# A third projection block behind the x loop, and the end of a search behind the fourth head

## The chip, the cores and the metric

The kernel runs on one core of a Trainium2 chip. A core has TensorE (PE, matmuls), VectorE (DVE), ScalarE (ACT), GpSimd (POOL) and SyncE (SP, which here issues nearly all DMAs); each works through its own queue in order, and they wait for each other by semaphores. The metric is device time in microseconds (us) of one execution.

## The reference

One inference step of a hybrid decoder layer, for 512 prompt tokens and 8 x 8 sample tokens (T = 576 in all), model width 2048. One projection feeds two branches: sparse attention, in which an indexer chooses the 256 keys each token may see, and gated linear attention (GLA). Both are gated and go through an output projection.

```python
def index_scores(qi, wi, ki):
    dots = jnp.einsum('bthd,bsd->btsh', qi, ki) * (D_IDX ** -0.5)
    return jnp.einsum('btsh,bth->bts', jax.nn.relu(dots), wi)
...
z = jnp.einsum('btd,de->bte', rms_norm(x, norm_in), w_in)        # split into q, k, v, gate, indexer q, k, w, GLA parts
_, idx = lax.top_k(jnp.where(causal, index_scores(qi, wi, ki), -jnp.inf), topk)
s = jnp.where(valid, q @ k[idx], NEG_BIG)                        # prompt: keys of the prompt
o = softmax(s) @ v[idx]                                          # sample: keys in a paged cache, and the new ones
y = rms_norm(x + concat([o * silu(ga), gla_out * silu(gb)]) @ w_out, norm_f)
```

## The kernel before

**Products.** All of it is float32, and each product is made of three matmuls of rounded parts: `w_hi*x_hi + w_lo*x_hi + w_hi*x_lo`. `wload` brings one weight piece (128 x 512, 256 KB): a DMA on SP into `w_raw` (3 buffers), a cast on ACT to `w_hi` (L180), a subtraction on DVE, in some stages on POOL, to `w_lo` (L183); `w_hi` and `w_lo` have 5 buffers each. `gemm(b)` projects 128 output columns from four such pieces: 16 slices of the model width, three products each. `kmm` makes all 576 tokens as two matmuls of 288 columns per product, `kmm_q` only 448 tokens in one matmul of 448 columns. Result tiles are `ps_g` (2 buffers of PSUM); `mm1` gives a tile of a second PSUM pool (`pm`, 3 buffers).

**Stages.** First the x loop (L272 on): x comes in 16 pieces, and blocks 0 (small columns: indexer key, indexer weights, GLA rank) and 1 (first indexer query) are accumulated as it comes. Behind it stands what depends on their sums: `raw0` copies block 0's sum out (L280), `rope64` swaps rows of block 1's sum into `ev_sw` by four copies on ACT (L293), the indexer key becomes `kih`/`kil` (L343, L344), and `pw` transposes the indexer weights on TensorE (L349). Then eight indexer blocks (`idx_block`), each with a query projection, `rope64` and six score matmuls `pq` (L419, L420). `squares` (L367) sums the squares of x, for the norm, on ACT: one 1 MB load `xt` and one instruction of 2048 columns per indexer block. Then heads 0 to 7 of the prompt attention (`head`): query, key, value and gate projections, scores, softmax, and `head_out` with transposes `pt`, the split `th`/`tl` (L721, L722), products `pv` and the gated result `ga` (L727). Heads 0 and 4 also project a group of values (`vgroup`).

**Work woven in.** The search for the top keys (prompt, then sample: `topk_sample`) is a generator `bg`, advanced a few steps at marked places of heads 0 to 3; what is left is drained behind head 3. Its end (L546 to L563) merges two halves of the sample search and writes the mask `biasS`. After that the tiles of the search give their memory to a pool in which `units` loads key and value pages (`kt`, `vt`, 5 tiles of four 256 KB loads) and computes the sample attention `pS`, `pOs` in pieces between the projections of heads 4 to 7. GLA, gates and the output projection follow.

**Order.** A scheduler, and not the program text alone, sets each engine's queue: it takes the instructions by priority and by its own model of times. `tc.high_priority(offset=WOFF)` puts weight loads ahead, `tc.issue_after(x)` keeps an instruction behind x in that order. `rounded` collects the `w_hi` casts, `ended` the last matmul of a chain.

Of the kernel before, what the change touches and what calls it, by code (L numbers as in the profile page):

```python
# [16 lines left out]
ALU = mybir.AluOpType  # L17
# [3 lines left out]
P = 128  # L21
# [98 lines left out]
def build(tc, I, O):  # L120
# [11 lines left out]
    def v2(ap):  # L132
        return ap.rearrange("p (j t) -> p j t", j=2)
# [67 lines left out]
    def split_x(k):  # L201
# [16 lines left out]
        xh.append(h)  # L218
        xl.append(l)

    def kmm(ps, k, hi, lo):
        wh = hi[:, (k % 4) * P : (k % 4 + 1) * P]
        wl = lo[:, (k % 4) * P : (k % 4 + 1) * P]
        for n, (wt, xt) in enumerate(((wh, xh[k]), (wl, xh[k]), (wh, xl[k]))):
            for j in range(2):
                pe.matmul(  # L226
                    ps[:, j, :HT], wt, xt[:, j * HT : (j + 1) * HT],
                    start=(k == 0 and n == 0), stop=(k == NK - 1 and n == 2),
                )

    def kmm_q(ps, k, hi, lo):
        c = slice((k % 4) * P, (k % 4 + 1) * P)
        for n, (wt, xt) in enumerate(((hi, xh[k]), (lo, xh[k]), (hi, xl[k]))):
            pe.matmul(ps[:, 0, :TQ], wt[:, c], xt[:, P:T], start=(k == 0 and n == 0), stop=(k == NK - 1 and n == 2))  # L234

    def gemm(b, mm=kmm, ps=None):
        if ps is None:
            ps = pg.tile([P, 2, 512], F32, name="ps_g", tag="ps_g")
        for half in range(2):
            for k0 in (8 * half, 8 * half + 4):  # L240
                hi, lo = wload(I["w"][b, :, k0 : k0 + 4, :])
                for k in range(k0, k0 + 4):
                    mm(ps, k, hi, lo)
            fill()
        return ps[:, :, :HT] if mm is kmm else ps[:, 0, :TQ]
# [10 lines left out]
    def mm1(name):  # L256
        return pm.tile([P, 512], F32, name=name, tag="pm")

    ended = []

    def run(first, *rest):
        lead = first()
        with tc.issue_after(getattr(lead, "ins", lead)), tc.high_priority(offset=WOFF):
# [10 lines left out]
    for k in range(NK):  # L274
        split_x(k)
        for b in range(2):
            _, hi, lo = first_w[b, k // 4]
            (kmm_q if b else kmm)(psf[b], k, hi, lo)
    raw0 = sm.tile([P, T], F32, name="raw0", tag="vaS")
    se.copy(v2(raw0), psf[0][:, :, :HT])  # L280
    ps0 = v2(raw0)

    ident = cload("ident", P, P)
# [5 lines left out]
    def rope64(ps):  # L289
        sw = ev.tile([P, TQ], F32, name="ev_sw", tag="e0", bufs=2)  # L290
        for q4 in range(4):
            d4 = q4 ^ 1
            se.copy(sw[32 * d4 : 32 * d4 + 32], ps[32 * q4 : 32 * q4 + 32])  # L293
        t1 = ev.tile([P, TQ], F32, name="ev_t1", tag="e1", bufs=2)
        ve.tensor_tensor(out=t1, in0=ps, in1=C64[:, P:T], op=ALU.mult)
        po_.tensor_tensor(out=sw, in0=sw, in1=S64[:, P:T], op=ALU.mult)
        ve.tensor_tensor(out=t1, in0=t1, in1=sw, op=ALU.add)
        return t1
# [47 lines left out]
    se.activation(v2(wiT), ps0[96:112], AF.Copy, scale=1.0 / 32.0)  # L346
    pw = mm1("pw")
    for i in range(1, 4):
        pe.transpose(pw[:, 16 * i : 16 * i + 16], wiT[:, P * i : P * (i + 1)], ident[0:16, 0:16])  # L349
    wtok = pa.tile([P, 48], F32, name="wtok")  # L350
    ve.tensor_copy(wtok, pw[:, 16:64])
    rstd = cp.tile([P, T], F32, name="rstd")
# [50 lines left out]
    sc = [None] + [pb.tile([P, (256, 384, 520)[i - 1]], F32, name=f"sc{i}", tag=f"sc{i}")[:, : P * (i + 1)] for i in range(1, 4)]  # L403

    def idx_block(blk):
        t1 = rope64(gemm(1 + blk, kmm_q, mm1("ps_q").rearrange("p (o n) -> p o n", o=1) if blk == 1 else None)) if blk else t1_first
        for e in range(2):
            hh = 2 * blk + e
            r = slice(64 * e, 64 * e + 64)
            rl_ = slice(64 - 64 * e, 128 - 64 * e)  # L410
            qs = pa.tile([P, TQ], F32R, name="qis", tag=("qis", "kch")[e], bufs=2)
            se.copy(qs[r], t1[r])
            ve.tensor_tensor(out=qs[rl_], in0=t1[r], in1=qs[r].bitcast(F32), op=ALU.subtract)
            po_.tensor_copy(qiS[:, :, hh, :], qs[:, TP - P :].bitcast(F32).rearrange("p (b t) -> p b t", t=DT))
            for i in range(1, 4):
                n = P * (i + 1)
                pq = mm1("pq")
                qc = slice(P * (i - 1), P * i)
                pe.matmul(pq[:, :n], qs[:, qc], kih[:, :n], start=True, stop=False)  # L419
                pe.matmul(pq[:, :n], qs[:, qc], kil[:, :n], start=False, stop=True)  # L420
                rl = pa.tile([P, 512], F32, name="rl", bufs=8)
                se.activation(rl[:, :n], pq[:, :n], AF.Relu)
                wcol = wtok[:, 16 * (i - 1) + hh : 16 * (i - 1) + hh + 1]
                if hh == 0:
                    ve.tensor_scalar(out=sc[i], in0=rl[:, :n], scalar1=wcol, scalar2=None, op0=ALU.mult)
                else:
                    ve.scalar_tensor_tensor(out=sc[i], in0=rl[:, :n], scalar=wcol, in1=sc[i], op0=ALU.mult, op1=ALU.add)

    for blk in range(8):
        idx_block(blk)  # L430
        if blk == 1:
            for to, src in ((ptab, "page_table"), (bm, "k_bm"), (gnorm, "gla_norm"), (bgate, "b_gate")):
                with tc.issue_after(wloads[-1]):
                    sy.dma_start(to, I[src])
        if blk == 6:
            raw = pr.tile([P, D], F32, name="xt", bufs=2)
            with tc.issue_after(wloads[-3]):
                sy.dma_start(raw[:, :512], I["k_sel"])
                sy.dma_start(raw[:, 512:960], I["k_lm"])
            po_.tensor_copy(selw, raw[:, :512])  # L440
            po_.tensor_copy(lm, raw[:, 512:960])
        if 0 < blk < 6:
            squares(blk - 1)
        if blk == 5:
            token_scales()
    for i in range(1, 4):
        n = P * (i + 1)
# [83 lines left out]
    def topk_sample():  # L531

        K = 256
        wk = pb.tile([P, T], F32, name="wk", tag="wk")[:, : 512 + DT]
        top = pb.tile([P, 256], F32, name="top", tag="sc1")
        turned = pb.tile([P, 384], F32, name="turned", tag="sc2")[:, :K]
        yield from topk(sS, K, wk, top, turned)
        far = pb.tile([P, K], F32, name="far")
        for r0 in range(0, P, 32):
            for to in (0, 16):  # L540
                sy.dma_start(far[r0 + to : r0 + to + 16], turned[r0 + 16 - to : r0 + 32 - to])

        u, cnt = wk[:, :K], pb.tile([P, 8], F32, name="cnt")
        by8 = lambda x: x.rearrange("p (r e) -> p e r", e=8)
        for e in range(8):
            ve.tensor_tensor(out=by8(u)[:, e], in0=by8(top)[:, e], in1=by8(far)[:, 7 - e], op=ALU.max)  # L546
        thr = cnt[:, 0:1]
        ve.tensor_reduce(out=thr, in_=u, op=ALU.min, axis=AX.X)

        for c, (src, op) in enumerate(((top, ALU.is_gt), (far, ALU.is_gt), (far, ALU.is_equal))):  # L550
            ve.tensor_scalar(out=u, in0=src, scalar1=thr, scalar2=None, op0=op)
            ve.reduce_sum(out=cnt[:, c + 1 : c + 2], in_=u, axis=AX.X)
        ve.scalar_tensor_tensor(out=cnt[:, 4:5], in0=cnt[:, 3:4], scalar=bm[:, 5:6], in1=cnt[:, 1:2], op0=ALU.mult, op1=ALU.add)
        ve.tensor_tensor(out=cnt[:, 4:5], in0=cnt[:, 4:5], in1=cnt[:, 2:3], op=ALU.add)
        ve.tensor_scalar(out=cnt[:, 4:5], in0=cnt[:, 4:5], scalar1=-1.0, scalar2=float(K), op0=ALU.mult, op1=ALU.add)
        rank = pb.tile([P, 520], F32, name="rank", tag="sc3")
        ve.tensor_scalar(out=wk, in0=sS, scalar1=thr, scalar2=None, op0=ALU.is_equal)
        ve.tensor_tensor_scan(out=rank, data0=wk, data1=wk, initial=0.0, op0=ALU.add, op1=ALU.max)
        ve.scalar_tensor_tensor(out=wk, in0=rank, scalar=cnt[:, 4:5], in1=wk, op0=ALU.is_le, op1=ALU.mult)
        ve.scalar_tensor_tensor(out=wk, in0=sS, scalar=thr, in1=wk, op0=ALU.is_gt, op1=ALU.add)  # L560
        ve.tensor_scalar(out=wk, in0=wk, scalar1=-1.0, scalar2=-NEG, op0=ALU.add, op1=ALU.mult)
        po_.tensor_copy(biasS[:, :512], wk[:, :512])
        ve.tensor_tensor(  # L563
            out=biasS[:, 512:].rearrange("p (b s) -> p b s", b=NB), in0=own.rearrange("p (b s) -> p b s", b=NB),
            in1=wk[:, 512:].unsqueeze(1).to_broadcast([P, NB, DT]), op=ALU.min,
        )
        yield
# [143 lines left out]
    def head_out(h, Pi, v, g1):  # L711
        vh, vl = v
        pv = mm1("pv")
        for j in range(4):
# [9 lines left out]
            pe.matmul(pv[:, P * j :], vh[:, vc], th[:, :n], start=(j == 0), stop=False)  # L724
            pe.matmul(pv[:, P * j :], vl[:, vc], th[:, :n], start=False, stop=False)
            pe.matmul(pv[:, P * j :], vh[:, vc], tl[:, :n], start=False, stop=(j == 3))
        ve.tensor_tensor(out=g1[:, :TP], in0=pv, in1=g1[:, :TP], op=ALU.mult)  # L727
        sy.dma_start(spill_a[h], g1[:, :TP])

    def head(h, bg, n):  # L730
# [160 lines left out]
    head(2, bg, 4)  # L891
    head(3, bg, 4)
    lo_eng[0] = ve
    for _ in bg:
        pass
    pb_s.close()
    pc_s.close()
    un, un_s = pool("unit", 1, side="right")
# [542 lines left out]
```

## Time and profile before

| | |
|---|---|
| median of 3 runs | 1231.33 us (1230.85 to 1232.21) |
| the profiled execution, and its span | 1230.99 us, 1229.2 us |
| granted TensorE clock, mean | 0.995 |
| busy in the span | PE 1210.2 us (98%), DVE 658.9, ACT 563.4, POOL 298.2 |
| chain that ended last | PE 91%, DVE 5%, ACT 2%, the rest 1% or less each |

The span is what the profile covers, 1.8 us less than the execution. A matmul's busy time overlaps the next one's, so TensorE's throughput is read from the distance between starts. A number in brackets behind a row is idle time before it, with the instruction that ended it. The granted clock is 1.00 at full speed (2.4 GHz) and 0.50 at half.

### The profile page before, as it was taken

To read this page: it belongs to the slowest core of one execution; us is meant where nothing else is said; L and a number is where in the kernel's file an instruction comes from. 1 tells how busy PE (TensorE), PEld (TensorE's weight loads), DVE (VectorE), ACT (ScalarE), POOL (GpSimd) and SP (SyncE) were. 2 spreads that over 40 slices of the span, in tenths; PEclk is the share of its full clock that TensorE was granted. 3 is DMA by queue.
4 is the path that set the end of the run, shared out by engine and by line. 5 is a ranking of instruction groups with operands and counts; after the bars stand their busy time and mean duration, and the time that the engine had idled before them with its cause. 6 is when DMAs were issued, how large, how long until landed. Compare 5 with 4: busy or idle time off the path is not lost.

```text
span 1229.2 us, 23550 instructions
## 1 busy us (share of the span) xinstructions
PE 1210.2 (98%) x8693; PEld 1073.7 (87%) x8693; DVE 658.9 (54%) x1328; ACT 563.4 (46%) x1077; POOL 298.2 (24%) x472
## 2 busy tenths in 40 slices
PE   8799999999999999999999999999999999999997
PEld 8799997899998779998888788788899998888897
DVE  6577899789863413444344535435465562323233
ACT  6686565445443423353334453445466542222234
POOL 1124656545420210100101420402223010101021
PEclk9899999999999999999999999999999999999999
DMA  9543334422376578656356693776425454334245
GB/s 312 171 152 98 100 90 113 158 78 93 102 258 206 178 257 282 226 167 228 113 199 228 219 339 125 265 256 218 151 83 188 152 167 140 103 103 122 80 125 176
DMA packets 127157, 209.55 MB, mean 170 GB/s; under 512 B 14513, under 2 KB 38082, under 8 KB 126338
## 3 DMA queue, kind: packets, MB, share of 16 engines
q1 hardware_dynamic: 125890, 206.50, 51.2%
q10 hardware_dynamic: 1152, 1.55, 0.4%
q8 instruction: 68, 1.11, 0.4%
q14 instruction: 47, 0.39, 0.1%
HBM read 184.65 MB, written 23.22 MB: 169 GB/s over the span
## 4 chain that ended last, share of the span: by engine, by line
PE 91%; DVE 5%; ACT 2%; issue 1%; DMA 1%; POOL 1%; SPq 0%; DVEq 0%; POOLq 0%; ACTq 0%
PE ps_g L226 38%; PE ps_g L234 6%; PE acc L1286 5%; PE acc L1284 5%; PE acc L1285 5%; PE ps_g L629 4%; PE ps_g L630 4%; PE ps_g L631 4%; PE pOs L265 2%; PE pS L265 1%; PE acc L1289 1%; PE acc L1288 1%; DVE wk L518 1%; PE ps_v L626 1%; PE ps_v L625 1%
## 5 line engine op out<-in xcount | busy, mean ns | idle before, releaser
L180 ACT CAST w_hi<-w_raw 128x512 fp32r<-128x512 f32 x316 | 193.9, 619 | 363.2 <-PE ps_g L226 122.7
L183 DVE TENSOR_TENSOR w_lo<-w_raw,w_hi 128x512 fp32r<-128x512 f32 x252 | 178.3, 710 | 322.9 <-ACT w_hi L180 314.5
L226 PE MATMUL ps_g<-xh,w_hi 128*128 128x288 f32 x1312 | 289.7, 299 | 0.5 <-ACT xh L215 0.5
L226 PE MATMUL ps_g<-xl,w_hi 128*128 128x288 f32 x1312 | 289.0, 299 | 0.0
L226 PE MATMUL ps_g<-xh,w_lo 128*128 128x288 f32 x1312 | 285.7, 297 | 0.0
L226 PEld LDWEIGHTS ps_g<-xh,w_hi 128*128 128x128 f32 x1312 | 213.6, 189 | 5.8 <-issue 1.7
L226 PEld LDWEIGHTS ps_g<-xl,w_hi 128*128 128x128 f32 x1312 | 213.3, 189 | 2.4 <-issue 1.2
L226 PEld LDWEIGHTS ps_g<-xh,w_lo 128*128 128x128 f32 x1312 | 212.3, 188 | 0.7
L1285 PE MATMUL acc<-w_lo,mh 128*128 128x512 f32 (+1 forms) x320 | 110.7, 346 | 0.0
L1286 PE MATMUL acc<-w_hi,ml 128*128 128x512 f32 (+1 forms) x320 | 110.7, 346 | 0.0
L1284 PE MATMUL acc<-w_hi,mh 128*128 128x512 f32 (+1 forms) x320 | 110.3, 346 | 0.0
L183 POOL TENSOR_TENSOR w_lo<-w_raw,w_hi 128x512 fp32r<-128x512 f32 x64 | 86.4, 1352 | 63.8 <-ACT w_hi L180 55.6
L629 PE MATMUL ps_g<-w_hi,xh 128*128 128x512 f32 x256 | 101.4, 397 | 0.2 <-DVE ev_t L592 0.2
L630 PE MATMUL ps_g<-w_lo,xh 128*128 128x512 f32 x256 | 100.4, 392 | 0.0
L631 PE MATMUL ps_g<-w_hi,xl 128*128 128x512 f32 x256 | 99.8, 390 | 0.0
L1285 PEld LDWEIGHTS acc<-w_lo,mh 128*128 128x128 f32 x320 | 60.5, 189 | 7.5
L1286 PEld LDWEIGHTS acc<-w_hi,ml 128*128 128x128 f32 x320 | 60.4, 189 | 7.5
L1284 PEld LDWEIGHTS acc<-w_hi,mh 128*128 128x128 f32 x320 | 60.4, 189 | 7.5
L1308 POOL TENSOR_TENSOR y<-y,nfb 128x512 f32<-128x512 f32 (+1 forms) x20 | 22.3, 1126 | 178.6 <-ACT yjk L1304 178.4
L629 PEld LDWEIGHTS ps_g<-w_hi,xh 128*128 128x128 f32 x256 | 48.1, 188 | 12.2 <-issue 1.7
L631 PEld LDWEIGHTS ps_g<-w_hi,xl 128*128 128x128 f32 x256 | 48.1, 188 | 9.9
L630 PEld LDWEIGHTS ps_g<-w_lo,xh 128*128 128x128 f32 x256 | 48.1, 188 | 9.7
(358 smaller groups left out, 1943.5 us busy)
## 6 DMA issues: line engine op xcount, KB each, us to landing
w_raw<-in_w SPq DMA_DIRECT2D x188, 256.0 KB, 3.0
kt<-in_ck SPq DMA_DIRECT2D x128, 256.0 KB, 5.2
vt<-in_cv SPq DMA_DIRECT2D x128, 256.0 KB, 5.3
w_raw<-in_wv SPq DMA_DIRECT2D x64, 256.0 KB, 3.0
w_raw<-in_wo SPq DMA_DIRECT2D x64, 256.0 KB, 2.7
xr<-in_xT SPq DMA_DIRECT2D x15, 288.0 KB, 4.9
xt<-in_xp SPq DMA_DIRECT2D x4, 1024.0 KB, 7.1
sv<-v_tok SPq DMA_DIRECT2D x16, 256.0 KB, 5.2
```

What stands on the lines that cost most here:

```text
L180: c = se.copy(hi, raw)
L183: lo_eng[0].tensor_tensor(out=lo, in0=raw, in1=hi.bitcast(F32), op=ALU.subtract)
L226: pe.matmul(ps[:, j, :HT], wt, xt[:, j * HT : (j + 1) * HT], start=(k == 0 and n == 0), stop=(k == NK - 1 and n == 2),)
L234: pe.matmul(ps[:, 0, :TQ], wt[:, c], xt[:, P:T], start=(k == 0 and n == 0), stop=(k == NK - 1 and n == 2))
L265: last = f()
L629: pe.matmul(accs[i], xh[k][:, c], wh, start=a, stop=False)
L630: pe.matmul(accs[i], xh[k][:, c], wl, start=False, stop=False)
L631: pe.matmul(accs[i], xl[k][:, c], wh, start=False, stop=b)
L1284: pe.matmul(acc, mh[k][:, tsl], wh, start=(k == 0), stop=False)
L1285: pe.matmul(acc, mh[k][:, tsl], wl, start=False, stop=False)
L1286: pe.matmul(acc, ml[k][:, tsl], wh, start=False, stop=(k == NK - 1))
L1308: po_.tensor_tensor(out=yc[:, :m], in0=yc[:, :m], in1=nfb[r, c0 : c0 + m], op=ALU.mult)
```

## The change

Two parts. In the first, the projection of block 2 (`gemm(2)`), which `idx_block(1)` used to ask for, is written directly behind the x loop. The copies `raw0` and `ev_sw` are kept behind the last cast of the block's weights (`rounded[-1]`), and the transposes `pw` behind the last matmul of the last `kmm_q` block (`ended[0]`). `squares`, `token_scales` and one load of constants move one indexer block later. In the second, `topk_sample` has four empty steps more, so that its end is left to the drain, and the drain is kept behind the last `ga` product (`px["end"]`), that of head 3.

```diff
+    ended = []
@@ kmm_q
-            pe.matmul(ps[:, 0, :TQ], wt[:, c], xt[:, P:T], start=(k == 0 and n == 0), stop=(k == NK - 1 and n == 2))
+            m = pe.matmul(ps[:, 0, :TQ], wt[:, c], xt[:, P:T], start=(k == 0 and n == 0), stop=(k == NK - 1 and n == 2))
+        ended[:] = [getattr(m, "ins", m)]
@@ behind the x loop
+    ps_next = gemm(2, kmm_q, mm1("ps_q").rearrange("p (o n) -> p o n", o=1))
     raw0 = sm.tile([P, T], F32, name="raw0", tag="vaS")
-    se.copy(v2(raw0), psf[0][:, :, :HT])
+    with tc.issue_after(rounded[-1]):
+        se.copy(v2(raw0), psf[0][:, :, :HT])
@@ rope64
-            se.copy(sw[32 * d4 : 32 * d4 + 32], ps[32 * q4 : 32 * q4 + 32])
+            with tc.issue_after(rounded[-1]):
+                se.copy(sw[32 * d4 : 32 * d4 + 32], ps[32 * q4 : 32 * q4 + 32])
@@ pw
-        pe.transpose(pw[:, 16 * i : 16 * i + 16], wiT[:, P * i : P * (i + 1)], ident[0:16, 0:16])
+        with tc.issue_after(ended[0]):
+            pe.transpose(pw[:, 16 * i : 16 * i + 16], wiT[:, P * i : P * (i + 1)], ident[0:16, 0:16])
@@ idx_block and the loop over it
-        t1 = rope64(gemm(1 + blk, kmm_q, mm1("ps_q").rearrange("p (o n) -> p o n", o=1) if blk == 1 else None)) if blk else t1_first
+        t1 = rope64(ps_next if blk == 1 else gemm(1 + blk, kmm_q)) if blk else t1_first
-        if blk == 6:
+        if blk == 7:
...
-        if 0 < blk < 6:
-            squares(blk - 1)
-        if blk == 5:
+        if 1 < blk < 7:
+            squares(blk - 2)
+        if blk == 6:
             token_scales()
@@ topk_sample
         yield from topk(sS, K, wk, top, turned)
+        for _ in range(4):
+            yield
@@ head_out
-        ve.tensor_tensor(out=g1[:, :TP], in0=pv, in1=g1[:, :TP], op=ALU.mult)
+        m = ve.tensor_tensor(out=g1[:, :TP], in0=pv, in1=g1[:, :TP], op=ALU.mult)
+        px["end"] = getattr(m, "ins", m)
@@ behind head(3, bg, 4)
-    for _ in bg:
-        pass
+    with tc.issue_after(px["end"]):
+        for _ in bg:
+            pass
```

In TensorE's queue before, the end of the x loop (`ps_g_102` and `ps_g_103` are the sums of blocks 0 and 1, `ps_g_698` is block 3):

```order
L226 MATMUL ps_g_102<-xl_408,w_hi_345 128x288 x2
L234 MATMUL ps_g_103<-xl_408,w_hi_351 128x448
L349 MATMUL pw_505<-c_ident_422,sS_503 128x16 x3
L234 MATMUL ps_g_698<-xh_120,w_hi_701 128x448
L234 MATMUL ps_g_698<-xh_120,w_lo_703 128x448
```

The same place now (`ps_q_420` is block 2, `ps_g_695` block 3), with block 2's last three slices left out:

```order
L228 MATMUL ps_g_102<-xl_408,w_hi_345 128x288 x2
L236 MATMUL ps_g_103<-xh_407,w_hi_351 128x448
L236 MATMUL ps_g_103<-xh_407,w_lo_352 128x448
L236 MATMUL ps_g_103<-xl_408,w_hi_351 128x448
L236 MATMUL ps_q_420<-xh_200,w_hi_441 128x448
L236 MATMUL ps_q_420<-xh_200,w_lo_443 128x448
...
L236 MATMUL ps_q_420<-xl_408,w_hi_477 128x448
L236 MATMUL ps_g_695<-xh_120,w_hi_698 128x448
L236 MATMUL ps_g_695<-xh_120,w_lo_700 128x448
L236 MATMUL ps_g_695<-xl_121,w_hi_698 128x448
L355 MATMUL pw_578<-c_ident_495,sS_576 128x16 x3
```

The 48 matmuls of block 2 stood behind the first `pq`; now 12 stand inside the x loop's last slices, 36 right behind it, and `pw` behind these and three of block 3.

In ScalarE's queue before, from the last cast within the x loop on:

```order
L180 CAST w_hi_586<-w_raw_584 128x512
L280 COPY raw0_420<-ps_g_102 128x576
L180 CAST w_hi_604<-w_raw_602 128x512
L293 COPY ev_sw_434<-ps_g_103 32x448 x4
L335 COPY ev_sw_491<-raw0_420 32x576
L336 COPY ev_sw_491<-raw0_420 32x576
L346 ACTIVATE sS_503<-raw0_420 16x576
L180 CAST w_hi_622<-w_raw_620 128x512
L367 ACTIVATE xt_695,sst_512<-xt_695 128x2048
L180 CAST w_hi_701<-w_raw_699 128x512
```

And now:

```order
L180 CAST w_hi_441<-w_raw_439 128x512
L180 CAST w_hi_459<-w_raw_457 128x512
L180 CAST w_hi_477<-w_raw_475 128x512
L180 CAST w_hi_698<-w_raw_696 128x512
L284 COPY raw0_493<-ps_g_102 128x576
L298 COPY ev_sw_507<-ps_g_103 32x448 x4
L340 COPY ev_sw_564<-raw0_493 32x576
L341 COPY ev_sw_564<-raw0_493 32x576
L351 ACTIVATE sS_576<-raw0_493 16x576
L180 CAST w_hi_716<-w_raw_714 128x512
```

All casts of block 2 and the first of block 3 (`w_hi_698`) now stand ahead of the copies; the square sum stands three casts later, ahead of `kih`.

In VectorE's queue now, behind head 3's `ga` (before, the rows L546 to L563 stood between the `tl` of head 2, ahead of that head's `ga`):

```order
L730 TENSOR_TENSOR tl<-pt,th 128x128
L183 TENSOR_TENSOR w_lo<-w_raw,w_hi 128x512
L735 TENSOR_TENSOR ga<-pv,ga 128x512
L554 TENSOR_TENSOR wk<-top,far 128x32 x8
L600 TENSOR_TENSOR ev_t_4824<-ps_g,c_c_1520 128x576
L556 TENSOR_REDUCE cnt<-wk 128x1
...
L569 TENSOR_SCALAR wk<-wk 128x520
L183 TENSOR_TENSOR w_lo<-w_raw,w_hi 128x512
L571 TENSOR_TENSOR biasS<-c_own,wk 128x64
L600 TENSOR_TENSOR ev_t_5015<-ps_g,c_c_1520 128x576
```

Between `ga` and `biasS` stand, besides the search's end, four `w_lo` and head 4's query (`ev_t_4824`, `ql`); head 4's key (`ev_t_5015`) follows. In SP's queue 20 `kt` loads now follow each other behind eight pieces of the value group's weights, where before they were spread between weight loads of head 3.

## Rows read from the trace of the kernel before

**Rows 1.** Waits of TensorE, whole span: engine, tile, line, releaser; us, times, longest
```profile
PE pw L349 <- ACT sS L346: 5.3, 1, 5.3
...
PE pv L726 <- DVE tl L722: 1.5, 1, 1.5
```
**Rows 2.** Timeline of TensorE, x loop's end: start, us, instruction, idle before, releaser
```profile
29.12 0.36 PE L234 MATMUL ps_g<-xl,w_hi 128*128 128x448 f32 x1
34.81 0.50 PE L349 MATMUL pw<-c_ident,sS 16*128 16x16 f32 x3 [5.33 <-ACT sS L346]
37.86 0.74 PE L234 MATMUL ps_g<-xh,w_hi 128*128 128x448 f32 x1 [2.55 <-ACT w_hi L180]
...
41.70 0.36 PE L234 MATMUL ps_g<-xh,w_hi 128*128 128x448 f32 x1
```
**Rows 3.** Windows: length; busy PE, PEld, DVE, ACT, POOL; granted clock; DMA share; GB/s
```profile
20.00:30.00 10.00, 9.49 (x60) 8.84 (x58) 6.66 (x13) 6.30 (x13) 0.00 (x0) 1.00 1.02 335
...
36.00:38.00 2.00, 0.14 (x1) 0.14 (x1) 1.17 (x3) 2.00 (x4) 0.00 (x0) 0.50 0.83 296
```
**Rows 4.** Timeline of ScalarE, same place
```profile
29.32 0.64 ACT L280 COPY raw<-ps_g 128x576 f32<-128x576 f32 x1 [3.22 <-PE ps_g L226]
...
30.55 2.13 ACT L293 COPY ev_sw<-ps_g 32x448 f32<-32x448 f32 x4
...
34.08 0.68 ACT L346 ACTIVATE sS<-raw 16x576 f32<-16x576 f32 x1
...
35.31 1.91 ACT L367 ACTIVATE xt<-xt 128x2048 f32<-128x2048 f32 x1
...
38.89 0.67 ACT L343 CAST kih<-wk 64x576 fp32r<-64x576 f32 x1
```
**Rows 5.** DMA issues, 18 to 50 us: KB each, median us to landing
```profile
xt<-in_xp SPq DMA_DIRECT2D x3, 1024.0 KB, 7.3
w_raw<-in_w SPq DMA_DIRECT2D x9, 256.0 KB, 4.5
```
**Rows 6.** Timeline of VectorE, the sample search's end
```profile
330.03 1.01 DVE L546 TENSOR_TENSOR wk<-top,far 128x32 f32<-128x32 f32 x7
...
343.29 0.23 DVE L563 TENSOR_TENSOR biasS<-c_own,wk 128x64 bf16<-128x64 f32 x1
```
**Rows 7.** Timeline of the DMA queue of SyncE: first page loads
```profile
346.10 1.41 SPq L157 DMA_DIRECT2D kt<-in_ck  x3
...
348.18 2.98 SPq L157 DMA_DIRECT2D kt<-in_ck  x5
```
**Rows 8.** Timeline of TensorE: projections, first page scores, head 3's last product
```profile
375.44 0.42 PE L226 MATMUL ps_g<-xh,w_hi 128*128 128x288 f32 x2
375.70 0.42 PE L226 MATMUL ps_g<-xh,w_lo 128*128 128x288 f32 x2
...
379.92 0.62 PE L262 MATMUL pS<-kt,qz 128*32 128x512 f32 x1
...
383.77 0.28 PE L726 MATMUL pv<-tl,vh 128*128 128x128 f32 x1
...
396.71 0.40 PE L629 MATMUL ps_g<-w_hi,xh 128*128 128x512 f32 x1
396.95 0.39 PE L630 MATMUL ps_g<-w_lo,xh 128*128 128x512 f32 x1
```
**Rows 9.** Windows while pages are loaded, columns as in Rows 3
```profile
346.00:352.00 6.00, 6.00 (x48) 6.00 (x47) 1.44 (x3) 2.51 (x4) 2.57 (x7) 1.00 0.70 237
352.00:356.00 4.00, 4.00 (x33) 4.00 (x32) 2.60 (x4) 1.25 (x2) 1.90 (x2) 1.00 1.03 391
```
**Rows 10.** DMA issues of the whole run
```profile
kt<-in_ck SPq DMA_DIRECT2D x128, 256.0 KB, 5.2
```
**Rows 11.** Windows of VectorE alone: length, busy (instructions), clock, DMA share, GB/s
```profile
150.00:160.00 10.00, 9.83 (x21) 1.00 0.16 49
```
**Rows 12.** Waits of VectorE from 236 to 252 us
```profile
DVE v_smp L665 <- ACT v_smp L664: 4.9, 1, 4.9
```

More of the change, by code (lines that the diff above doesn't have):

```diff
@@ L257, in mm1 @@
         return pm.tile([P, 512], F32, name=name, tag="pm")
-    ended = []
     def run(first, *rest):
```

## The prediction

> **What bounds the kernel now.** TensorE. The page's first part has it busy 1210.2 of 1229.2 us, and its chain of waits gives 91% to TensorE, so a change in another engine's work counts only where TensorE stands still. I then read TensorE's waits, largest first: 5.3 us at `pw`, further down 1.5 us at a `pv` of head 2 [rows 1]. The reader should see how few they are: two places, and the change touches both. Around the first I read TensorE's timeline and the windows, around the second VectorE's timeline, and then the page loads, because they start when the sample search is over.
>
> At the end of the x loop the last matmul starts at 29.12, `pw` at 34.81, the next projection at 37.86 [rows 2]. In between the granted clock falls from 1.00 to 0.50 [rows 3]. Releaser is ScalarE both times, which was not idle but at work in its order: `raw0`, four `ev_sw` copies, two more, `sS`, a square sum of 1.91 us, and only then the cast that TensorE wants [rows 4].
>
> **The first part.** Matmul spacing comes from neighbouring starts: 0.26 us for two of 288 columns [rows 8], so 0.20 for one of 448.
> - The gap. The x loop's successor could start at 29.32; the projection starts at 37.86 [rows 2]. Of these 8.5 us `pw` itself keeps about 0.2 in its new place (its row has 0.50 at half clock). Removed: 8.3.
> - The slow start. From 37.86 to 41.70 ten matmuls start, so nine spacings in 3.84 us where full clock needs 1.8 [rows 2]. With no gap ahead of them there is no reason for the clock to fall. Removed: 2.0.
> - No matmul is added or taken away; block 2's 48 are only moved. They last 9.8 us: 12 within the x loop, 36 behind it, so that the x loop ends near 31.8 and `pw` comes near 39.8.
>
> What must be ready in that time? The pieces of block 2 are cast as they land. SP's queue now has the 1 MB `xt` load behind the weights of block 3, where it stood ahead of the last of block 2, so the median landing of 4.5 us [rows 5] leaves 2 to 3 us of slack. ScalarE copies from about 32.4: 0.64 and 2.13 us, two copies and `sS` of 0.7 each [rows 4], so `sS` is ready near 37.2, TensorE asks at 39.8. That stall is gone. Late next is the end of the same queue: three casts, the square sum (1.91), then `kih` (twice 0.67) [rows 4]. The third cast needs a weight piece queued behind the 1 MB `xt` (median 7.3 us [rows 5]); issued near 34, it lands at 39 to 41. `kih` is ready at 43.5 to 45, the first `pq` asks near 45.6. Behind `kih` stand the four copies of block 2's sum, which holds one of only three buffers of the second PSUM pool; the third `pq` needs it. That is 2.1 us of copies, a cast and 0.6 us on VectorE: ready at 47.5 to 49, asked for near 48.5. I take 0.5 us of new wait; bounds 0 and 3 (a landing that late shifts the whole queue).
>
> Moving `squares` and `token_scales` back one block changes no work. In the windows TensorE is busy 9.49 of 10 us in the x loop [rows 3]; the 12 matmuls put there may fill those holes, worth 0 to 0.5 on the good side; I count 0.
>
> **Does the gain survive?** VectorE is nearly full from 150 to 236 us (9.83 of 10 in the first window [rows 11]), so TensorE could run into it. But before 150 it idles behind the indexer blocks and will get its work earlier with them, and it has 4.9 us in hand at `v_smp` behind that stretch [rows 12]. If it did not move forward at all, 10.3 - 4.9 = 5.4 us would come back; taken: 0.
>
> **The second part.** The wait at `pv` of head 2 is 1.5 us [rows 1]: VectorE is working off the search's end between that head's `tl`. Removed: 1.5. The price is paid later, in sequence:
> - The search's end runs from 330.03 to 343.52 [rows 6]; five other instructions in it take 2.3, so 11.2 us are its own.
> - Head 3's last `pv` starts at 383.77 [rows 8]. It moves up by 11.8, and by 3.6 because the sixteen page matmuls (from 379.92 [rows 8]) now stand behind it; about 1.5 us of projections stand ahead instead. So it ends near 370.0.
> - VectorE: 370.0 + `ga` 0.6 + 11.2 + 5.2 for the four `w_lo`, two `ev_t` and `ql` between gives `biasS` near 387. The mask's first use on TensorE is near 388.5 by the queue. Little slack.
> - Memory for the pages comes free then: the first `kt` load was issued at 346.10 [rows 7], 2.6 us after `biasS`; now it is at about 387, 41 us later.
> - TensorE now has 28.8 us of matmuls between that `pv` and the first page matmul (86 of 288 columns at 0.13, 69 of 512 at 0.23, the small `pq`), so it asks near 398.8. The first matmul takes the last page tile, so all sixteen loads must be there.
> - Sixteen loads are 4.19 MB. At 391 GB/s [rows 9] they take 10.7 us: 397.7 and a little. By SP's pace, 0.6 us per load [rows 7], the last is issued near 396 and lands 5.2 us later [rows 10]: 401.2. Wait between 0 and 2.5 us; I take 1.5.
> - The later fetches have 13 to 20 us between buffer release and need. The tightest, twelve `vt` loads, needs 12 x 0.6 + 5.2 = 12.4 against 13.4: 0.3 us.
>
> The Trainium skill, "DMA: Bandwidth & Descriptors" (section "Where 436 GB/s comes from"), says that a load from HBM is held to about 358 GB/s per core. By that the sixteen loads would take 11.7 us, the wait 2.5 and the sum 1.0 more. Here the row has 391 over 4 us, so it does not hold in this trace, and the sum goes by the row.
>
> **Sum.** 1230.99 - 8.3 - 2.0 - 1.5 + 0.5 + 1.5 + 0.3 = 1220.5 for the profiled execution. The median lies 0.34 above it, so 1220.8. My terms for new waits are the middle of their bounds with three margins of 1 to 2 us unproved; I add 0.7 and forecast 1221.5, 0.8% faster.
>
> **Rivals.**
> 1. Pages come late. For it: the margins above, and 41 us of lead gone. A burst that meets the value weights costs 2 to 3 us at the first scores, and as much at the first `pOs` and at the second scores: 4 to 6 us above the forecast, about 1226. Against: 391 GB/s while both streams run [rows 9].
> 2. VectorE holds TensorE between 150 and 240, up to 5.4 us come back: 1226. For it: the full windows [rows 11]; against: its idle time ahead of them.
> 3. The change doesn't do what it says: block 2's later pieces land late in a queue whose share is already 1.02 [rows 3], or the third `pq` waits for its buffer, 3 us and with it part of the slow start: 1226 to 1229.
> 4. Slower. The page loads run at 237 GB/s, as in the first window [rows 9], instead of 391. The first sixteen then take 17.7 us, TensorE waits 8.4 at the first scores, and each of the next three fetches (3.1 MB, 13.3 us and landing) misses its window by 2 to 5: 16 to 18 in all against 11.8 won, so 1235 to 1238. It decides from 14.3 us of new waits on. Against: in that window SP was still issuing weights between pages, and the next one has 391.
>
> A long new wait would cost more than itself: behind the gap of 8.5 us here, 2.0 more were lost at clock 0.50 [rows 2, 3]. The Trainium skill, "TensorE: Matmul & The Clock Gate" (Part 1), states the same: idle time throttles the array, and activity releases it. No row here shows a fall behind a wait of 1 to 3 us, and I add nothing for one.
>
> **How the numbers follow.** Forecast 0.62, rival 1 0.14, rival 2 0.07, rival 3 0.09, rival 4 0.05; 0.03 for a gain beyond it (all new waits 0 and the holes of the x loop filled: 1218.5). About 0.2%, 2.5 us, is what a measurement of this kernel can tell from no change. Rivals 1 and 2 are still faster by more, half of rival 3 too: faster 0.89, same 0.06, slower 0.05. The range is 1218 to 1228; it leaves out rival 4 and the end of rival 3. The likeliest case alone is 1219 to 1224.
>
> **What would show it.** Right: no wait of TensorE between 29 and 45, the clock 1.00 there, block 2's matmuls ending near 39.7; no wait at `pv` near 330; `biasS` near 387, first `kt` behind it, and a wait of 0 to 2.5 at the first page matmul near 399. Wrong: a wait at `pq` of the first block above 2 us, waits of `ps_g` on VectorE near 180 to 230, or page waits that repeat at each `pS` and `pOs`.

## The result, and the profile after

The changed kernel takes 1220.22 us (median of 6, 1219.71 to 1220.51) beside 1231.09 for the kernel before in the same runs: ratio 0.991, interval 0.9897 to 0.9923. Forecast were 1221.5 and a range of 1218 to 1228. The profiled execution has a span of 1218.4 us, 10.8 less than before.

First the page of the changed kernel: its span, and TensorE's busy time.

```profile
span 1218.4 us, 23549 instructions
...
PE 1208.4 (99%) x8687; PEld 1073.0 (88%) x8693; DVE 651.7 (53%) x1328; ACT 563.4 (46%) x1077; POOL 296.0 (24%) x472
```

TensorE idles 10.0 us instead of 19.0, and its busy time is 1.8 less though no matmul was dropped: that is the slow start. Then its waits, all that are listed:

```profile
PE ps_idle L273 <- DVE sst L365: 1.1, 1, 1.1
PE ps_g L637 <- DVE ev_t L600: 0.6, 1, 0.6
PE pU L398 <- ACT w_hi L180: 0.4, 1, 0.4
PE pO L1147 <- DVE Sst L1155: 0.3, 1, 0.3
PE pS L263 <- issue: 0.3, 2, 0.2
PE pt L726 <- DVE p L715: 0.3, 1, 0.3
PE pl L263 <- DVE mxs L835: 0.3, 1, 0.3
```

`pw` and `pv` of [rows 1] are gone, the first page scores (`pS`) do not wait for a DMA, and the longest wait is the one at the kernel's start. In TensorE's timeline, where [rows 2] had two gaps:

```profile
31.20 0.36 PE L236 MATMUL ps_g<-xl,w_hi 128*128 128x448 f32 x1
31.40 0.36 PE L236 MATMUL ps_q<-xh,w_hi 128*128 128x448 f32 x1
...
39.10 0.37 PE L236 MATMUL ps_g<-xl,w_hi 128*128 128x448 f32 x1
39.40 0.35 PE L355 MATMUL pw<-c_ident,sS 16*128 16x16 f32 x3
39.68 0.47 PE L236 MATMUL ps_g<-xh,w_hi 128*128 128x448 f32 x1
...
45.47 0.46 PE L425 MATMUL pq<-kih,qis 128*128 128x256 f32 x2
```

The x loop ends at 31.20 and block 2 follows at the normal spacing of 0.20; `pw` costs 0.4. In the windows of that stretch, against [rows 3], TensorE is full and its clock granted in full:

```profile
20.00:30.00 10.00, 10.00 (x61) 9.51 (x60) 6.98 (x13) 6.07 (x12) 0.00 (x0) 1.00 0.85 283
...
36.00:38.00 2.00, 2.00 (x12) 1.85 (x11) 1.39 (x2) 1.95 (x4) 1.02 (x1) 1.00 0.09 23
```

ScalarE's timeline shows what TensorE no longer waits for, in the order of [rows 4]:

```profile
30.53 0.62 ACT L180 CAST w_hi<-w_raw 128x512 fp32r<-128x512 f32 x1 [0.99 <-DMA w_raw<-in_w]
31.05 0.63 ACT L284 COPY raw<-ps_g 128x576 f32<-128x576 f32 x1
...
35.25 0.68 ACT L351 ACTIVATE sS<-raw 16x576 f32<-16x576 f32 x1
...
40.61 1.35 ACT L348 CAST kih<-wk 64x576 fp32r<-64x576 f32 x2
...
43.59 1.07 ACT L298 COPY ev_sw<-ps_q 32x448 f32<-32x448 f32 x2
```

`sS` is ready at 35.9, 3.5 us before `pw`; `kih` at 42.0, 3.5 us before the first `pq`; the last copy of block 2's sum at 44.7. ScalarE is as busy as before (563.4 us in both kernels), but TensorE has other work meanwhile.

The second place in the changed kernel: VectorE's mask, the first page load in SP's queue, and the first page matmul.

```profile
383.28 0.63 DVE L571 TENSOR_TENSOR biasS<-c_own,wk 128x64 bf16<-128x64 f32 x1
```
```profile
384.27 12.06 SPq L157 DMA_DIRECT2D kt<-in_ck  x20
```
```profile
398.82 0.62 PE L263 MATMUL pS<-kt,qz 128*32 128x512 f32 x1
```

The mask is done at 383.9, 3 us earlier than forecast, and the sixteenth load is issued near 393.6 (fifteen steps of 0.62). By an estimate with the median of 4.7 us from issue to landing in that stretch it lands near 398.3: half a microsecond to spare.

### The profile page after: what moved, and what is told of

Its sections match the earlier page's. It is cut to its first block, busy times and chain, and to the rows that moved or that the text cites. A ratio compares the mean times of both kernels' runs of the same rounds, so it can differ in the third digit from the quotient of the medians.

```text
span 1218.4 us, 23549 instructions
## 1 busy us (share of the span) xinstructions
PE 1208.4 (99%) x8687; PEld 1073.0 (88%) x8693; DVE 651.7 (53%) x1328; ACT 563.4 (46%) x1077; POOL 296.0 (24%) x472
## 4 chain that ended last, share of the span: by engine, by line
PE 92%; DVE 3%; DMA 1%; issue 1%; ACT 1%; SPq 1%; POOL 0%; DVEq 0%; ACTq 0%; POOLq 0%
PE ps_g L228 39%; PE ps_g L236 6%; PE acc L1296 5%; PE acc L1294 5%; PE acc L1295 5%; PE ps_g L637 4%; PE ps_g L638 4%; PE ps_g L639 4%; PE pOs L266 2%; PE pS L266 2%; PE acc L1299 1%; PE acc L1298 1%; PE ps_v L633 1%; PE ps_v L634 1%; PE ps_q L236 1%
## 5 line engine op out<-in xcount | busy, mean ns | idle before, releaser
L637 PEld LDWEIGHTS ps_g<-w_hi,xh 128*128 128x128 f32 x256 | 48.1, 188 | 10.9 <-DVE ev_t L600 1.0
```

The source lines that it names most:

```text
L637: pe.matmul(accs[i], xh[k][:, c], wh, start=a, stop=False)
```

## Experiments

Ratios are to the kernel before on the same chip; "under" and "over" are in us of the medians.

**Each part alone.** The change's diff, one half undone at a time.

> Only the first part: block 2 behind the x loop; the end of the sample search stays where it was, ahead of the third head's gated product. If the parts add up as the two traces suggest, the stall behind the x loop (gap 8.3, slow start 2.0) and the two small waits in the x loop (about 0.9) go, and a wait of VectorE's search near head 2 stays (1.5): 9.0 to 9.6 us under the kernel before, 1221.5 to 1222. Rival: with TensorE 10 us earlier VectorE is later by comparison, the wait at the third head's pv grows from 1.5 to 3 or more, and the gain is 7 to 8 us.

1221.47 beside 1231.56 (0.991, 0.9897 to 0.9924): 10.1 under.

> Only the second part: the search's end behind the fourth head, the x loop's end as before. If the parts add up: the wait of 1.5 us at pv goes and nothing takes its place, 1.2 to 1.6 us under the kernel before, near 1229.6. Rival: the first part's earlier start is what makes room for it, and alone the late pages cost as much as the wait did: 0 to 0.5 us. The first page matmuls should show no wait above 0.5 us by the theory, 1 to 2 us by the rival.

1230.51 beside 1231.56 (0.9989, 0.998 to 0.9998): 1.05 under. No wait at `pv`, none above 0.5 at the pages.

The parts add up to 11.1, and the whole change gave 10.9. By the ratios the first part alone (0.991) cannot be told from the whole change (0.991); that the second part adds to it shows in the waits, not in the time. Neither rival held. The gains miss their ranges by half a microsecond or less, the first above (10.1 for 9.0 to 9.6), the second below (1.05 for 1.2 to 1.6). In the first run the wait at `pv` did not grow but shrank, from 1.5 to 0.7, with the second part undone:

```profile
PE pv L732 <- DVE tl L728: 0.7, 1, 0.7
```

So on top of the first part the second is worth less than its row in the waits said. In the second run the profile gains only 0.2 although the 1.5 us are gone from its waits. One cause is in its window behind the x loop's end (columns as in Rows 3):

```profile
42.00:44.00 2.00, 2.00 (x8) 1.85 (x7) 0.69 (x1) 0.82 (x2) 0.00 (x0) 0.52 0.00 0
```

After the same gap (8.7 us from the x loop's last matmul to the next projection in both) the clock is at half nearly until 44, where the kernel before had 1.00 from 42 on. What a gap costs behind itself varies between executions, here by about 1 us (half of the 2 us or so by which the half clock lasts longer).

**The place of `pw`.**

```diff
-    ps_next = gemm(2, kmm_q, mm1("ps_q").rearrange("p (o n) -> p o n", o=1))
...
-        with tc.issue_after(ended[0]):
-            pe.transpose(pw[:, 16 * i : 16 * i + 16], wiT[:, P * i : P * (i + 1)], ident[0:16, 0:16])
+        m = pe.transpose(pw[:, 16 * i : 16 * i + 16], wiT[:, P * i : P * (i + 1)], ident[0:16, 0:16])
+    pw_last = getattr(m, "ins", m)
+
+    def kmm_late(ps, k, hi, lo):
+        with tc.issue_after(pw_last):
+            kmm_q(ps, k, hi, lo)
+
+    ps_next = gemm(2, kmm_late, mm1("ps_q").rearrange("p (o n) -> p o n", o=1))
```

The holds on `raw0` and `ev_sw` are left out here as well.

> The changed kernel with one thing turned round: the transposes pw stand ahead of block 2's 48 matmuls on TensorE, not behind them, and the copies of the first sums stand between the casts as before. If the stall was TensorE's place in line behind pw (theory), TensorE waits for sS again, about 5 to 6 us behind the x loop's last matmul, but no second time for a cast, since the pieces of block 2 are cast by then; the clock falls in the gap and the next 4 us run at half: 7 to 8 us over the changed kernel, near 1228. Rival: what mattered was the weights' casts ahead of the copies in ScalarE's queue; then most of the loss is the second wait and the whole of the old time comes back, 10 us, near 1230.5.

1228.86 (0.9977, 0.9966 to 0.9987): 2.7 under the kernel before, some 8 over the changed one. TensorE's timeline of this run:

```profile
28.78 0.36 PE L236 MATMUL ps_g<-xl,w_hi 128*128 128x448 f32 x1
35.07 0.50 PE L351 MATMUL pw<-c_ident,sS 16*128 16x16 f32 x3 [5.93 <-ACT sS L348]
35.49 0.74 PE L236 MATMUL ps_q<-xh,w_hi 128*128 128x448 f32 x1
...
39.02 0.51 PE L236 MATMUL ps_q<-xh,w_hi 128*128 128x448 f32 x1
```

One wait instead of two: the 2.6 us for the cast are won, the 5.9 at `pw` and the slow start (nine spacings in 3.53 us, 1.7 lost) stay. That is the theory's split: most of the gain goes when `pw` stands first again. What matters most is that TensorE has 7 us of block 2's matmuls between the x loop and the first instruction that needs ScalarE's chain.

The holds on order were no part of it: the changed kernel without `issue_after` on `raw0`, `ev_sw` and `pw` is the same program, instruction by instruction on all five engines. Asking for block 2 ahead of them in the program was enough.

**The square sums back in their place.**

```diff
-        if blk == 7:
+        if blk == 6:
...
-        if 1 < blk < 7:
-            squares(blk - 2)
-        if blk == 6:
+        if 0 < blk < 6:
+            squares(blk - 1)
+        if blk == 5:
             token_scales()
```

> The changed kernel with the sums of squares (and what follows from them) one indexer block earlier, where they stood before. The 1 MB load of x then stands ahead of block 2's last piece again and the 1.9 us square sum ahead of block 3's first cast. Theory: block 2's 36 matmuls cover it, TensorE waits 0 to 0.5 us, same time within 1 us (1220 to 1221). Rival: the load comes late, ScalarE stands still behind it, and block 3's first matmuls or pw wait 1 to 3 us: 1221.5 to 1223.5.

1221.71 (0.9915, 0.9902 to 0.9929): 0.6 over the changed kernel by the ratios, whose intervals overlap. The profiled execution took 1224.84, the longest of five and 3.1 above their median, so its rows show what can happen and not the usual size. They are on the rival's side; ScalarE, then TensorE, and two windows behind the wait:

```profile
34.84 0.62 ACT L180 CAST w_hi<-w_raw 128x512 fp32r<-128x512 f32 x1 [4.21 <-DMA w_raw<-in_w]
```
```profile
40.76 0.47 PE L236 MATMUL ps_g<-xh,w_hi 128*128 128x448 f32 x1 [1.72 <-ACT w_hi L180]
41.48 0.66 PE L236 MATMUL ps_g<-xh,w_lo 128*128 128x448 f32 x1 [0.25 <-DVE w_lo L183]
...
45.18 0.37 PE L236 MATMUL ps_g<-xl,w_hi 128*128 128x448 f32 x1
```
```profile
42.00:43.00 1.00, 1.00 (x4) 0.92 (x3) 0.00 (x0) 0.95 (x3) 0.84 (x1) 0.50 0.46 119
...
44.00:45.00 1.00, 1.00 (x5) 0.87 (x4) 0.97 (x3) 0.98 (x2) 0.00 (x0) 0.50 0.02 8
```

With the 1 MB load ahead of it, block 2's last piece lands 4 us after ScalarE wants it, everything behind it is late, and TensorE waits 1.7 us at block 3. Behind the wait the granted clock falls from 1.00 to 0.50: the ten spacings from 41.48 to 45.18 take 3.70 us, 1.7 more than ten of 0.20. So in this execution the late piece costs some 3.4 us, half of it in clock. The prediction knew no row of a fall behind a wait of 1 to 3 us and added nothing for one; this is such a row.

**A later mask.** One pass of the search's end done 9 times instead of once (8 more, about 4 us; the expectation's ten is a slip), and 19 times in the second run:

```diff
-        ve.tensor_scalar(out=wk, in0=sS, scalar1=thr, scalar2=None, op0=ALU.is_equal)
+        for _ in range(9):
+            ve.tensor_scalar(out=wk, in0=sS, scalar1=thr, scalar2=None, op0=ALU.is_equal)
```

> The changed kernel with about 4 us more of work on VectorE (ten more passes over 520 columns, which leave the result as it is) within the search's end, so that the mask, and with it the first page load, is 4 us later. The scheduler knows of it and moves the first page matmuls some 40 rows down TensorE's queue, about 6 us. Theory: since the consumer moves with its model of the loads, TensorE does not wait more than 1 us for pages, and the time stays within 1 us of the changed kernel. Rival (pages late, as in the prediction): each late microsecond is paid at the first scores, 3 to 4 us more.

1219.88 beside 1232.24 (0.99, 0.9884 to 0.9915): nothing lost.

> The same with about 8 us more. Theory: still within 1 us; head 4's key split may now wait on VectorE, 0.5 to 1.5 us more. Rival: 7 to 8 us more, twice the run with 4 us.

1221.3 (0.991, 0.9895 to 0.9925): nothing that can be measured. The mask comes at 390.3 and 398.2, which is 6.4 and 14.3 us later than in the changed kernel and more than meant, since other work slipped in between. The first page matmul stands at 408.9 and 416.9 instead of 398.8:

```profile
L263 PE MATMUL pS<-kt,qz x16: 592/605/617, 408.9 to 792.1; 128*32 128x512 f32 x16
```
```profile
L263 PE MATMUL pS<-kt,qz x16: 592/605/617, 416.9 to 794.0; 128*32 128x512 f32 x16
```

The consumer moves with the mask, because the scheduler places it by its own model of the loads. Late pages are not paid where the scheduler knows that they are late. The prediction's rivals 1 and 4 speak of pages that come later than the scheduler expects, which these two runs do not test.

**GpSimd beside VectorE.** Why was the mask at 383.9 and not at 387? In the kernel before, some instructions of the search's end are long. VectorE, and then GpSimd, in the same stretch:

```profile
335.06 0.92 DVE L553 SCALAR_TENSOR_TENSOR cnt<-cnt,bm 128x1 f32<-128x1 f32 x1
...
336.31 1.39 DVE L554 TENSOR_TENSOR cnt<-cnt 128x1 f32<-128x1 f32 x1
...
338.93 1.79 DVE L559 SCALAR_TENSOR_TENSOR wk<-rank,cnt,wk 128x520 f32<-128x520 f32 x1
```
```profile
334.68 1.29 POOL L183 TENSOR_TENSOR w_lo<-w_raw,w_hi 128x512 fp32r<-128x512 f32 x1 [2.48 <-ACT w_hi L180]
335.98 1.70 POOL L593 TENSOR_TENSOR ev_sw<-ev_sw,c_s 128x576 f32<-128x576 f32 x1
```

The two instructions on a single column end at 335.98 and 337.70, when a GpSimd instruction ends (335.97 and 337.68). In the changed kernel GpSimd is nearly idle at that place, and the same three take 0.22, 0.15 and 0.75.

> The changed kernel with head 4's first weight splits w_lo left on GpSimd instead of VectorE. Fewer instructions stand in VectorE's queue between the fourth head's product and the mask (4 w_lo of 0.7 us go), but GpSimd now reads SBUF beside it. Theory, from the kernel before, where single VectorE instructions of the search's end took 0.9 to 1.8 us and ended with a GpSimd instruction: two-input instructions of the search's end grow again to 0.9 or more when they meet a w_lo on GpSimd, and the search's end gains less than the 2.7 us taken out of it. Rival: the long ones before were something else (waits on their own inputs), they stay as short as in the changed kernel (0.15 to 0.8). Time within 1 us of the changed kernel either way.

1222.32 (0.992, 0.9905 to 0.9936). It did not do what it was meant to: all `w_lo` of that stretch stayed on VectorE, and GpSimd none the busier there. GpSimd made eight `w_lo` more than in the changed kernel, but the last at 363.4, ahead of the search's end, and a new wait of 1.6 us came at a `pv` of head 4, at 469.9. Nothing follows for the question.

So GpSimd was loaded by hand, beside the search's end of the changed kernel, with reading products in one run (shown) and with ten memsets in the other (`see` is a copy of the threshold):

```diff
         ve.tensor_reduce(out=thr, in_=u, op=ALU.min, axis=AX.X)
+        scr = pb.tile([P, 512], F32, name="scr")
+        see = pb.tile([P, 1], F32, name="see")
+        ve.tensor_copy(see, thr)
+        po_.memset(scr, 0.0)
+        po_.tensor_copy(scr[:, :1], see)
+        for _ in range(4):
+            po_.tensor_tensor(out=scr, in0=scr, in1=rstd[:, :512], op=ALU.mult)
```

> The changed kernel with four products of 128x512 on GpSimd (into a tile nobody reads, about 1.3 us each) beside the search's end, released by its threshold; VectorE's queue is the same but for one copy of a column. Theory (GpSimd instructions that read SBUF hold up VectorE's): instructions of the search's end that take 0.15 to 0.8 us become up to 1.3 us longer, each ending with a GpSimd product, and the mask comes 2 to 5 us later than 383.9. Rival: the long instructions in the kernel before had another cause; every one keeps its time and the mask comes at 384 to 384.5. The time stays within 1 us of the changed kernel unless head 4's key is held up too.

> The same with ten memsets of that tile (0.5 us each, about as long in sum), which only write. If GpSimd's reading is what holds VectorE up, nothing grows and the mask comes within 0.5 us of the changed kernel's; if any busy GpSimd does, it looks like the run with the products.

1224.82 and 1221.19 us, two executions each beside 1231.2. VectorE and GpSimd with the products:

```profile
380.57 0.75 DVE L568 SCALAR_TENSOR_TENSOR cnt<-cnt,bm 128x1 f32<-128x1 f32 x1
...
381.64 1.25 DVE L569 TENSOR_TENSOR cnt<-cnt 128x1 f32<-128x1 f32 x1
...
387.13 0.63 DVE L578 TENSOR_TENSOR biasS<-c_own,wk 128x64 bf16<-128x64 f32 x1
```
```profile
376.73 6.14 POOL L563 TENSOR_TENSOR scr<-scr,rstd 128x512 f32<-128x512 f32 x4
```

And with the memsets:

```profile
378.69 0.22 DVE L567 SCALAR_TENSOR_TENSOR cnt<-cnt,bm 128x1 f32<-128x1 f32 x1
...
379.45 0.14 DVE L568 TENSOR_TENSOR cnt<-cnt 128x1 f32<-128x1 f32 x1
...
383.90 0.63 DVE L577 TENSOR_TENSOR biasS<-c_own,wk 128x64 bf16<-128x64 f32 x1
```
```profile
376.21 6.11 POOL L562 MEMSET scr<- 128x512 f32 x10
```

Both keep GpSimd busy for 6.1 us over the same instructions. Beside the products the two single-column instructions take 0.75 and 1.25 and end at 381.3 and 382.9, which are the ends of the third and fourth product (1.53 each from 376.73); beside the memsets they take 0.22 and 0.14. The Trainium skill, "SBUF — State Buffer" (section "SBUF: two separate sides"), states this: a VectorE instruction with two SBUF inputs and a GpSimd instruction that reads SBUF take one port pair by turns, each for its whole length, while one that only writes is no rival for it. These rows agree. Not all that grew fits this sentence: beside the products two passes with one tile and one column as inputs (L566, 128x256) took 1.20 and 0.94 instead of 0.36 and 0.35, and one beside the memsets (L571, 128x520) 0.70 instead of 0.49. What held these is not shown. The mask beside the memsets is 0.6 us later than in the changed kernel, 0.3 of it because the search's end starts later.

The run with the products shows something else. Its mask is 3.2 us later than beside the memsets (0.5 of it because all ahead of it is), and the order of TensorE and VectorE is the same in both. One of its waits, a window behind it, and the 27 page matmuls that follow, first beside the products and then beside the memsets:

```profile
PE pS L263 <- DMA kt<-in_ck: 2.4, 1, 2.4
```
```profile
404.00:405.00 1.00, 1.00 (x8) 0.27 (x4) 0.00 (x0) 0.00 (x0) 0.00 (x0) 0.50 1.05 406
```
```profile
402.60 4.88 PE L266 MATMUL pS<-kt,qz 128*32 128x512 f32 x27
```
```profile
399.99 3.18 PE L266 MATMUL pS<-kt,qz 128*32 128x512 f32 x27
```

So a mask that the scheduler does not foresee as late is paid for: 2.4 of 2.7 us in the wait, and 1.7 more because the granted clock falls to 0.50 behind it. The two are most of the 4.4 us by which this execution's span (1222.8) exceeds the changed kernel's; the expectation had the time within 1 us. Not every such wait costs clock: behind the 1.5 us at `pv` in the kernel before and the 1.6 us at head 4's `pv` in the run above the granted clock stayed at 1.00.

**Another way to the second part.** In the kernel before, one line moved, so that head 3's `w_lo` go to VectorE and GpSimd is quiet beside the search's end:

```diff
+    lo_eng[0] = ve
     head(3, bg, 4)
-    lo_eng[0] = ve
```

> The kernel before with one line moved: the weight splits w_lo go from GpSimd to VectorE one head earlier, ahead of the fourth head. Tells what made VectorE late at the third head's tl. Theory: it was the order in VectorE's queue together with instructions held up by GpSimd; with GpSimd quiet the wait of 1.5 us at pv goes, so about 1.2 to 1.5 us under the kernel before without moving the search's end. Rival: VectorE was simply full there, the extra w_lo (0.7 us each) make it later still, the wait grows to 2 us or more: 0.5 us or more over the kernel before.

1230.25 beside 1232.24 (0.9983, 0.9974 to 0.9992): 2.0 under, no wait at `pv`, though VectorE has more to do. The order of its queue also changes here (the last `tl` now stands ahead of the long instructions), so the run does not tell order from hold-ups.

> The first part with the one moved line in place of the second: w_lo on VectorE from the fourth head on, the search's end where it was before. If the two gains are separate, the 10.1 us of the first part and the rest of the wait at pv (0.7 left there) add up: 0.5 to 1 us under the first part alone, level with the changed kernel (its ratio to the kernel before within 0.001 of 0.991). Rival: with the w_lo on VectorE the wait grows instead, 0.5 us or more over the first part alone.

1219.33 beside 1231.2 (0.9904, 0.9889 to 0.9919): level with the changed kernel (0.991), as expected; its median is the lowest of all, by less than the intervals can tell.

> The changed kernel with the same line moved as well. Theory: both remove the same wait, so nothing is added: within 0.5 us of the changed kernel. Rival: GpSimd's w_lo hold up VectorE elsewhere in the fourth head too, and another 0.5 to 1 us goes.

1220.09 (0.9911, 0.9897 to 0.9924): nothing on top. The line and the second part remove the same wait.

## Why the prediction was right

- *The gap, 8.3.* Right: 8.5 less `pw`'s 0.4 is 8.1. The copies and casts ran as placed, `sS` 1.3 us earlier than estimated.
- *The slow start, 2.0.* Right in the mechanism: clock 1.00 throughout and busy time down by 1.8. Where the gap was left (`pw` first, the second part alone) it came back with 1.7 to about 3 us.
- *Holes in the x loop, counted at 0, bound 0.5.* A misreading, without effect on the sum: there were none. The 0.51 us that 9.49 lacks are the gap's beginning, since the x loop's last matmul ends at 29.48 and the window at 30.00. Block 2's next matmul does start 0.4 us early, at 31.40 for 29.32 + 2.44 = 31.76, but this lead is there at 17 us already, six us ahead of block 2's first matmul. It comes from waits of the kernel before at the x loop's beginning, between 5 and 8 us:

```profile
PE ps_g L234 <- DVE w_hi L198: 0.5, 1, 0.5
PE ps_g L226 <- ACT xh L215: 0.5, 2, 0.3
```

  In the profiled executions of the other runs such waits add up to anything from 0 to 1.7 us, with the change and without it. That the changed kernel's profile has none is luck.
- *`pq` and its chain, 0.5.* Too high by 0.5: no wait. The weight piece behind the 1 MB load came in time, and `kih` was done 1.5 us ahead of my early estimate.
- *VectorE full from 150, taken 0.* Right: one wait of 0.6 there (`ps_g` on `ev_t`) where there was 0.2. The 10 us survived.
- *The wait at `pv`, 1.5.* Gone, but the first part alone takes half of it away, so the second adds less than its row.
- *Pages, 1.5.* This step failed in size: measured 0. The queue's times were right (the first page matmul at 398.8 as worked out, the search's start near 370.3), but the search's end was carried over from its old place with 11.2 us, and 2.0 of these were not its own: the same instructions took 9.2 where GpSimd was nearly quiet (13.6 from 370.3 to 383.9, less 4.4 for the four `w_lo`, two `ev_t` and `ql`, which I had at 5.2). The other 1.1 are 0.8 of these seven instructions and 0.3 of an earlier start. With the mask at 387.8, near the forecast, the run with the products paid 2.4 us of wait, inside the bounds of 0 to 2.5, and 1.7 of clock, for which the prediction had added nothing. That the pages cost nothing was luck: an early mask, and not the margin that was worked out.
- *Sum.* The recorded line has a slip: 1230.99 - 8.3 - 2.0 - 1.5 + 0.5 + 1.5 + 0.3 is 1221.5, not 1220.5, so with 0.34 and 0.7 the terms give 1222.5, 2.3 above the measured time and still inside the range. The slip of 1.0 brought the forecast nearer by luck. What the two profiles show: of TensorE's waits 5.3 and 2.6 at the gap, 1.5 at `pv` and 1.0 at the x loop's beginning are gone, 10.4 in all; 1.4 are new (`ps_g` 0.4 more, `pU` 0.4, `pO` 0.3, `pS` 0.3); with 1.8 less of busy time that is 10.8, as measured. The terms were too high because of the new waits (2.3 for 1.4) and the 0.7 on top. Two smaller slips decide nothing: the chances for faster add up to 0.905, not 0.89, and rival 4's wait at the first scores is 5.9 by its own figures (387 + 17.7 - 398.8), not 8.4.
- *Rivals.* Rival 2 shows in no run. What rival 3 feared, a late piece of block 2 and part of the slow start, shows in one, with the square sums back in their place: 1.7 of wait and 1.7 of clock. The move of the 1 MB load guards against it. Rival 1 shows in the run with the products, once and not at the later scores, and 4.1 us in all. Rival 4 did not come: from 392 to 400 us the changed kernel loads at 391 to 395 GB/s.

Open: why the first part alone shortens the wait at `pv`. Its search instructions are held up too, at other places than before; that GpSimd's phase against VectorE's shifted is likely, and was not tested.

## What to carry to other kernels

Where one engine is full, look for the few places at which it stands, and put independent work of its own between producer and consumer there; the work in the other engines' queues need not get faster. Asking for that work earlier in the program can be all it takes, and it pays twice when the idle time also costs clock, as it did here behind 8.5 us and, in two executions, behind 1.7 and 2.4. And do not carry an instruction's duration to a new place without looking at what the neighbour engine did beside it in the old one.

## What was not expected of the hardware

A VectorE instruction on one column (0.15 us) can last 1.4 us when GpSimd reads SBUF beside it, and keeps its time beside memsets (0.14). After the same gap (8.5 us without work for it but `pw`) TensorE ran at half clock until about 41.6 in one execution and nearly until 44 in another. A wait of 1.7 us was followed by some 3 us at half clock in one execution, while behind waits of 1.5 and 1.6 us elsewhere the clock stayed full.
